# Three extra 8-column matmuls in a gated attention and mLSTM layer

## The chip, the cores and the metric

The kernel runs on 1 core of one Trainium2 chip. The metric is the device time of one execution in microseconds (us); less is better. The TensorE clock granted in the profiled execution was 0.999 of full speed.

## What is computed

One layer of a hybrid network on 256 tokens of width 1024, in float32. The input is normalized and modulated to `h`, and one large product `h @ w_in` gives 13 pieces: attention's queries, keys, values and gate input `za`; the mixer's (mLSTM's) `qm`, `km`, `vm`, `zm`, `om` and its two small gates; and the two output gates `ga` and `gm`. Cut to what matters here:

```python
h = _rmsnorm(x, norm_w) * (1 + scale) + shift
(qa, ka, va, za, qm, km, vm, zm, om, ig, fg, ga, gm) = jnp.split(h @ w_in, SPLIT_IDX, axis=-1)
ya = merge(_moba_attention(qa, ka, heads(va, ATT_HEADS), rel_bias))
ya = (ya * jax.nn.silu(za)) @ w_att_proj
...
ym = (merge(hm).astype(x.dtype) * jax.nn.silu(zm)) @ w_ml_proj
y = jax.nn.sigmoid(ga) * ya + jax.nn.sigmoid(gm) * ym
return x + gate * (y @ w_out)
```

## The kernel before

**The products.** Each float32 operand is split into a high part (`wh`, `hTh`) that TensorE's one-pass float32 format (`F32R`) holds exactly, and a low part (`wl`, `hTl`) with the rest. A product is then three matmuls: high by high, high by low, low by high. ScalarE (ACT) makes `wh` from the loaded block (line 449), VectorE (DVE) or GpSimd (POOL) makes `wl` by a subtraction (line 453).

**The chunks.** After a first phase (lines up to 300) the work is a list of chunks of 512 output columns, two per piece ("halves"), in the order ka, va, za, qm, km, att, zm, vm, om, ga, gm, ml, out. A chunk has 4 steps, which I call groups; a group covers 2 of the 8 blocks of 128 rows over which the product sums. There are two kinds of interest:

- "tok" chunks (lines 1087 to 1089) stream 512 columns of weights for each loaded block of `h`;
- "ws" chunks (za, qm, km, att, ga, gm, ml; lines 1094 to 1097) load a 128 by 128 block of weights and stream the 256 tokens of `h`. For each of the 2 blocks of the sum and each of 4 column blocks `i`, three matmuls stand in a row: `wh` with `hTh` (line 1094), `wh` with `hTl` (line 1096), `wl` with `hTh` (line 1097). That is 24 matmuls a group, each with its own weight load (LDWEIGHTS).

**The order.** The order on every engine is written out by hand: at step `g` the loop over groups first splits the weights of a later group (`HB` = 5 buffers ahead), then runs the hooks that are listed for that step, then issues the group's matmuls. Hooks put other work of TensorE between groups: attention's scores and transposes (lines 695, 696, 720 to 722) and its products with the values (733, 735) ahead of groups of va, za and the first groups of qm; the mixer's products (852 to 854) ahead of the second, third and fourth group of ga; transposes of the mixer's result (892) ahead of gm's first group and ahead of the first group of its second half. I call such a piece an interlude. The result of a ws chunk goes to a PSUM tile `mm` of 128 by 4 by 256 words, one slice for each `i`, with two such tiles in turn.

Of the kernel before, what the change touches and what calls it, by code (L numbers as in the profile page):

```python
# [64 lines left out]
def tile_hybrid(ctx: ExitStack, tc: tile.TileContext, x, c, params, params2, rel_t, w_row, ada_mod, ada_gate,  # L65
                w_in, w_att_proj, w_ml_proj, w_out, out):
    nc = tc.nc
# [212 lines left out]
    for step in P1_STEPS:  # L280
        op, k = step[0], int(step[1])
# [16 lines left out]

    chunks = []

    STRASSEN = ('zm', 'om')

    def seg(kind, src, c0, name, stat=None):
        if name in STRASSEN:
            chunks.append(dict(kind="str", src=src, c0=c0, half=0, n=512, name=name, stat=stat))
            return
        for hf in range(2):
            chunks.append(dict(kind=kind, src=src, c0=c0, half=hf, n=512, name=name, stat=stat))
# [20 lines left out]
    NG = len(owner)  # L329
    for nm in STRASSEN:  # L330
        C[nm, 1] = C[nm, 0]

    def start(name, half=0):
        return step0[C[name, half]]

    def done(name, half):
        return step0[C[name, half]] + (14 if name in STRASSEN else 4)

# [119 lines left out]
    def at(step, fn, *a):  # L458
        hooks.setdefault(step, []).append((fn, a))
# [527 lines left out]
    for i, j in enumerate((0, 1, 2, 3)):  # L987
        at(start("qm") + 2 + 4 * i, left_split, j)
    for nm in STRASSEN:
        s = start(nm)  # L990
# [4 lines left out]
    for hp in range(2):  # L995
        s = done("om", hp)
        if "om" in STRASSEN:
            for i in range(2):
# [17 lines left out]
    mmt = {}  # L1016
# [16 lines left out]
    for g in range(NG):  # L1033
        ci = owner[g]
        kp = g - step0[ci]
        ch = chunks[ci]
# [29 lines left out]
        sh_, sl_ = (hTh, hTl) if ch["stat"] is None else (T[stat[ch["stat"]][0]], T[stat[ch["stat"]][1]])  # L1066
        wh, wl = whl[g]
        if ci == NCH - 1:
            continue
        if ch["kind"] == "str":  # L1070
            p = kp // 2
            o = mmt[ci][(0, 2, 0, 1, 0, 2, 0)[p]]
            for kk in range(2):
                k = 2 * (kp % 2) + kk
# [5 lines left out]
        for kk in range(2):  # L1080
            k = 2 * kp + kk
            first, last = k == 0, k == KT - 1
            if ch["kind"] == "tok":
                for t in range(2):
                    a, b = sh_[:, k, t * 128:(t + 1) * 128], sl_[:, k, t * 128:(t + 1) * 128]
                    o = mmt[ci][:, t, 0:ch["n"]]
                    nc.tensor.matmul(o, a, wh[:, kk], start=first, stop=False)  # L1087
                    nc.tensor.matmul(o, a, wl[:, kk], start=False, stop=False)  # L1088
                    nc.tensor.matmul(o, b, wh[:, kk], start=False, stop=last)  # L1089
            else:  # L1090
                for i in range(4):
                    cs = slice(i * 128, (i + 1) * 128)
                    o = mmt[ci][:, i]
                    nc.tensor.matmul(o, wh[:, kk, cs], sh_[:, k], start=first and i % 2 == 0, stop=False,  # L1094
                                     skip_group_check=True)
                    nc.tensor.matmul(o, wh[:, kk, cs], sl_[:, k], start=False, stop=False, skip_group_check=True)  # L1096
                    nc.tensor.matmul(o, wl[:, kk, cs], sh_[:, k], start=False, stop=last and i % 2 == 1,  # L1097
                                     skip_group_check=True)
    ci = NCH - 1
    for t, c0, n in ((0, 0, 512), (1, 0, 256), (1, 256, 256)):  # L1100
        pt = ps.tile([128, n], F32, name="mm", bufs=2)
        for k in range(KT):
            wh, wl = whl[step0[ci] + k // 2]
            wh, wl = wh[:, k % 2, c0:c0 + n], wl[:, k % 2, c0:c0 + n]
# [52 lines left out]
```

## Time and profile before

| | |
|---|---|
| median of 3 runs | 350.89 us (350.68 to 351.04) |
| the profiled execution | 350.94 us |
| its span, first to last instruction | 349.2 us |
| TensorE matmuls busy | 343.6 us, 2320 matmuls and as many weight loads |
| VectorE, ScalarE, GpSimd busy | 270.7, 228.1, 104.9 us |
| matmuls in ws chunks | 1344 of 256 columns (320 + 64 + 64 at each of lines 1094, 1096, 1097) |

The busy time of a matmul in the profile overlaps that of its neighbours, since matmuls are pipelined; a row's duration of 276 ns does not mean that a matmul takes a slot of 276 ns. What a matmul costs in a stream is the distance from its start to the next one's start, and this is read from the timeline's start column.

### The profile page before, as it was taken

What the parts mean: (1) busy time and instruction counts of PE and PEld (TensorE: products, weight loads), DVE (VectorE), ACT (ScalarE), POOL (GpSimd) and SP (SyncE); (2) the same over time, 40 slices, a digit from 0 to 9 for tenths busy, and PEclk for the clock granted to TensorE, in tenths of its full rate; (3) what the DMA queues carried; (4) which work ended last, traced back from release to release, by engine and by line L of the source; (5) the groups of instructions that cost most, each with busy time, mean ns of one, the idle gap of its engine ahead of it and who ended that gap; (6) DMA issues with size and microseconds to landing.
All of it is one profiled execution on the core that took longest, in us unless ns stands there. A gap on an engine that the chain in (4) does not pass through costs nothing.

```text
span 349.2 us, 6004 instructions
## 1 busy us (share of the span) xinstructions
PE 343.6 (98%) x2320; PEld 315.0 (90%) x2320; DVE 270.7 (78%) x392; ACT 228.1 (65%) x355; POOL 104.9 (30%) x102
## 2 busy tenths in 40 slices
PE   8999999999999999999999999999999999999995
PEld 4988889888999999999999888888899999999885
DVE  4799994897984445668699897999966889888772
ACT  3777787989977678676644985469956425834410
POOL 4940003765202999744714000100003440000000
PEclk9999999999999999999999999999999999999999
DMA  8999999995483063275398484957969029746011
GB/s 299 418 419 420 417 381 344 243 259 229 140 286 122 11 246 129 98 287 198 103 333 167 158 326 145 363 95 274 387 231 354 20 94 321 312 174 249 0 62 60
DMA packets 26782, 80.05 MB, mean 229 GB/s; under 512 B 2045, under 2 KB 5121, under 8 KB 26242
## 3 DMA queue, kind: packets, MB, share of 16 engines
q1 hardware_dynamic: 25392, 77.03, 61.2%
q0 software_dynamic: 1056, 2.10, 3.5%
q10 hardware_dynamic: 306, 0.55, 0.5%
q8 instruction: 18, 0.29, 0.3%
q14 instruction: 10, 0.08, 0.1%
HBM read 78.22 MB, written 1.45 MB: 228 GB/s over the span
## 4 chain that ended last, share of the span: by engine, by line
PE 82%; DMA 8%; POOL 4%; DVE 2%; ACT 2%; issue 1%; SPq 0%; DVEq 0%; POOLq 0%; ACTq 0%
PE mm L1094 15%; PE mm L1097 15%; PE mm L1096 15%; DMA raw<-in_w_row_dram 8%; PE pm L186 4%; PE mm L1087 4%; PE mm L1089 4%; PE mm L1088 4%; PE aux L1076 4%; PE aux L1077 4%; PE aux L1078 4%; POOL ms L572 2%; PE mm L1108 1%; PE mm L1106 1%; PE mm L1107 1%
## 5 line engine op out<-in xcount | busy, mean ns | idle before, releaser
L453 DVE TENSOR_TENSOR wl<-raw,wh 128x1024 fp32r<-128x1024 f32 (+1 forms) x96 | 118.4, 1255 | 32.6 <-ACT wh L449 32.5
L449 ACT CAST wh<-raw 128x1024 fp32r<-128x1024 f32 (+1 forms) x104 | 104.7, 1031 | 26.4 <-PE mm L1096 15.1
L1094 PE MATMUL mm<-hTh,wh 128*128 128x256 f32 x320 | 89.9, 281 | 0.0
L1097 PE MATMUL mm<-hTh,wl 128*128 128x256 f32 x320 | 89.0, 278 | 0.0
L1096 PE MATMUL mm<-hTl,wh 128*128 128x256 f32 x320 | 89.0, 278 | 0.0
L1094 PEld LDWEIGHTS mm<-hTh,wh 128*128 128x128 f32 x320 | 60.4, 189 | 0.0
L1097 PEld LDWEIGHTS mm<-hTh,wl 128*128 128x128 f32 x320 | 60.3, 188 | 0.0
L1096 PEld LDWEIGHTS mm<-hTl,wh 128*128 128x128 f32 x320 | 60.2, 188 | 0.0
L1087 PE MATMUL mm<-wh,hTh 128*128 128x512 f32 (+1 forms) x96 | 36.3, 378 | 0.0
L1089 PE MATMUL mm<-wh,hTl 128*128 128x512 f32 (+1 forms) x96 | 35.7, 372 | 0.0
L1088 PE MATMUL mm<-wl,hTh 128*128 128x512 f32 (+1 forms) x96 | 35.7, 372 | 0.0
L1089 PEld LDWEIGHTS mm<-wh,hTl 128*128 128x128 f32 x96 | 18.0, 188 | 3.2
L1088 PEld LDWEIGHTS mm<-wl,hTh 128*128 128x128 f32 x96 | 18.1, 188 | 2.9
L1087 PEld LDWEIGHTS mm<-wh,hTh 128*128 128x128 f32 x96 | 18.0, 188 | 2.8
L453 POOL TENSOR_TENSOR wl<-raw,wh 128x1024 fp32r<-128x1024 f32 x8 | 20.0, 2533 | 0.0
L175 DVE TENSOR_TENSOR wrl<-raw,wrh 128x512 fp32r<-128x512 f32 (+1 forms) x24 | 18.2, 778 | 1.6 <-ACT wrh L170 1.3
L1094 PE MATMUL mm<-yah,wh 128*128 128x256 f32 x64 | 17.9, 279 | 0.0
L170 ACT CAST wrh<-raw 128x512 fp32r<-128x512 f32 (+1 forms) x24 | 15.8, 685 | 3.1 <-DMA raw<-in_w_row_dram 3.1
L1096 PE MATMUL mm<-yal,wh 128*128 128x256 f32 x64 | 17.7, 276 | 0.0
L1097 PE MATMUL mm<-yah,wl 128*128 128x256 f32 x64 | 17.7, 276 | 0.0
L1097 PE MATMUL mm<-ymh,wl 128*128 128x256 f32 x64 | 17.7, 276 | 0.0
L1094 PE MATMUL mm<-ymh,wh 128*128 128x256 f32 x64 | 17.7, 276 | 0.0
(237 smaller groups left out, 773.6 us busy)
## 6 DMA issues: line engine op xcount, KB each, us to landing
raw<-in_w_in_dram SPq DMA_DIRECT2D x36, 1024.0 KB, 5.4
adat<-in_ada_mod_dram SPq DMA_DIRECT2D x16, 512.0 KB, 9.4
raw<-in_w_att_proj_dram SPq DMA_DIRECT2D x4, 1024.0 KB, 5.0
gw<-in_ada_gate_dram SPq DMA_DIRECT2D x4, 1024.0 KB, 8.6
raw<-in_w_ml_proj_dram SPq DMA_DIRECT2D x4, 1024.0 KB, 7.5
raw<-in_w_out_dram SPq DMA_DIRECT2D x4, 1024.0 KB, 8.9
raw<-in_w_row_dram SPq DMA_DIRECT2D x4, 896.0 KB, 12.6
raw<-in_w_row_dram SPq DMA_DIRECT2D x4, 640.0 KB
```

The costliest lines, as they stand in the source:

```text
L170: copy(wsp[k][0][:, c0:c1], wrow[k][:, c0:c1])
L175: e.tensor_tensor(l[:, cs], wrow[k][:, cs], h[:, cs].bitcast(F32), op=OP.subtract)
L186: nc.tensor.matmul(pm[ch][:, t], a[:, k, t * 128:(t + 1) * 128], b[:, cs], start=k == 0 and i == 0 and (ch < 3 or t == 0), stop=k == KT - ...
L449: nc.scalar.copy(h, w)
L453: e.tensor_tensor(l, w, h.bitcast(F32), op=OP.subtract)
L1076: nc.tensor.matmul(o, a, wh[:, kk], start=k == 0 and p in (0, 1, 3), stop=False, skip_group_check=True)
L1087: nc.tensor.matmul(o, a, wh[:, kk], start=first, stop=False)
L1088: nc.tensor.matmul(o, a, wl[:, kk], start=False, stop=False)
L1089: nc.tensor.matmul(o, b, wh[:, kk], start=False, stop=last)
L1094: nc.tensor.matmul(o, wh[:, kk, cs], sh_[:, k], start=first and i % 2 == 0, stop=False, skip_group_check=True)
L1096: nc.tensor.matmul(o, wh[:, kk, cs], sl_[:, k], start=False, stop=False, skip_group_check=True)
L1097: nc.tensor.matmul(o, wl[:, kk, cs], sh_[:, k], start=False, stop=last and i % 2 == 1, skip_group_check=True)
```

## The change

A table names three pieces and a position for each. In the first half of such a piece, at the first of its 96 matmuls (`k` = 0, `i` = 0), one more matmul is issued: the same weights `wh`, and the first 8 of the 256 columns of `hTh`. In za it stands ahead of the first matmul and writes to the first 8 words of slice 0; in ga behind the first, in gm behind the second, both into the first 8 words of slice 2. Each of these words is started afresh by a later matmul, so nothing of the extra product stays in the result.

```diff
+    EXTRA = {'za': 1, 'ga': 2, 'gm': 3}
...
                     o = mmt[ci][:, i]
+                    extra = EXTRA.get(ch["name"]) if first and i == 0 and ch["half"] == 0 else None
+                    if extra == 1:
+                        nc.tensor.matmul(o[:, 0:8], wh[:, kk, cs], sh_[:, k, 0:8], start=True, stop=True,
+                                         skip_group_check=True)
                     nc.tensor.matmul(o, wh[:, kk, cs], sh_[:, k], start=first and i % 2 == 0, stop=False,
                                      skip_group_check=True)
+                    if extra == 2:
+                        nc.tensor.matmul(mmt[ci][:, 2, 0:8], wh[:, kk, cs], sh_[:, k, 0:8], start=True, stop=True,
+                                         skip_group_check=True)
                     nc.tensor.matmul(o, wh[:, kk, cs], sl_[:, k], start=False, stop=False, skip_group_check=True)
+                    if extra == 3:
+                        nc.tensor.matmul(mmt[ci][:, 2, 0:8], wh[:, kk, cs], sh_[:, k, 0:8], start=True, stop=True,
+                                         skip_group_check=True)
                     nc.tensor.matmul(o, wl[:, kk, cs], sh_[:, k], start=False, stop=last and i % 2 == 1,
                                      skip_group_check=True)
```

The added lines shift the numbers below them: lines 1094, 1096, 1097 of before are 1099, 1104, 1108 of the changed kernel, and lines between the table and there move by one. The other engines' instructions and waits stay as they are, and so do the waits on TensorE.

TensorE at the start of za, in the changed kernel: behind the three transposes of attention (`aux<-ident,P`) the extra matmul (128x8) is the first of the chunk.

```order
L721 MATMUL aux<-ident,P 128x128 [waits DVE_49,Activation_49]
L722 MATMUL aux<-ident,P 128x128
L723 MATMUL aux<-ident,P 128x128
L1097 MATMUL mm<-hTh,wh 128x8
L1099 MATMUL mm<-hTh,wh 128x256
L1104 MATMUL mm<-hTl,wh 128x256
L1108 MATMUL mm<-hTh,wl 128x256
```

In the kernel before, the row of line 1097 with 128x8 is not there, and the others stand in the same order. None of the ws rows has a wait there.

TensorE at the start of gm's first half, before: eight transposes of the mixer's result (the last two shown as one row), then the chunk's matmuls. Only the first waits (for ACT, which makes `wh`).

```order
L892 MATMUL aux<-ident,omt 128x128 [waits DVE_49]
L892 MATMUL aux<-ident,omt 128x128 x2
L1094 MATMUL mm<-hTh,wh 128x256 [waits Activation_49]
L1096 MATMUL mm<-hTl,wh 128x256
L1097 MATMUL mm<-hTh,wl 128x256
```

And the same place in the changed kernel:

```order
L893 MATMUL aux<-ident,omt 128x128 [waits DVE_49]
L893 MATMUL aux<-ident,omt 128x128 x2
L1099 MATMUL mm<-hTh,wh 128x256 [waits Activation_49]
L1104 MATMUL mm<-hTl,wh 128x256
L1106 MATMUL mm<-hTh,wh 128x8
L1108 MATMUL mm<-hTh,wl 128x256
```

The extra matmul has gone between the second and the third, and no wait has moved. For comparison, the first group of gm's second half, which the change does not touch, starts like this in the kernel before: its third matmul does wait (for DVE, which makes `wl`).

```order
L892 MATMUL aux<-ident,omt 128x128 x8
L1094 MATMUL mm<-hTh,wh 128x256 [waits Activation_49]
L1096 MATMUL mm<-hTl,wh 128x256
L1097 MATMUL mm<-hTh,wl 128x256 [waits DVE_49]
L1094 MATMUL mm<-hTh,wh 128x256
```

In ga the extra matmul stands between the first (which waits for ACT) and the second matmul of the chunk, behind a last matmul of om with 512 columns.

## The prediction, on record before the changed kernel ran

> **What bounds the kernel now.** First the page's line of busy times, then the list of what TensorE (PE) waited for, then the timeline's last rows.
>
> ```profile
> PE 343.6 (98%) x2320; PEld 315.0 (90%) x2320; DVE 270.7 (78%) x392; ACT 228.1 (65%) x355; POOL 104.9 (30%) x102
> ```
>
> ```profile
> PE warm L213 <- POOL ident masks.py:199: 1.4, 1, 1.4
> PE pc L220 <- DMA xnT<-in_c_dram: 0.3, 1, 0.3
> ```
>
> ```profile
> 345.54 0.42 DVE L932 TENSOR_TENSOR o<-mm,gateb 128x256 f32<-128x256 f32 x1 [1.99 <-PE mm L1108]
> ```
>
> TensorE is busy all the time, waits for nobody beyond the first few microseconds, and its last matmul releases the last evacuation. So the time is the sum of TensorE's slots, and a slot saved or added anywhere from 12 us on is saved or added at the end: no other engine covers it, and none comes late when TensorE gains a few tenths (no wait of its own is left to grow).
>
> The rest of the argument is about the length of a slot. I read how many ws matmuls start in stretches of 10 us without an interlude (the windows view: the stretch, its length, busy time and count of matmuls, of weight loads, of DVE, ACT and POOL, then the granted clock and the DMA share).
>
> ```profile
> 147.00:157.00 10.00, 10.00 (x91) 10.00 (x90) 7.05 (x13) 6.81 (x11) 5.26 (x3) 1.00 0.66 246
> 279.00:289.00 10.00, 10.00 (x88) 10.00 (x87) 8.47 (x11) 3.21 (x7) 3.84 (x1) 1.00 0.32 108
> ```
>
> The same instructions, at the same granted clock (1.00), run at two rates. Starts of whole groups of 24 matmuls, from the timeline, give the sizes: in gm's first half (281.22 on) and in its second (293.32 on).
>
> ```profile
> 281.22 0.28 PE L1094 MATMUL mm<-hTh,wh 128*128 128x256 f32 x1
> ...
> 284.05 0.28 PE L1094 MATMUL mm<-hTh,wh 128*128 128x256 f32 x1
> ```
>
> ```profile
> 293.32 0.28 PE L1094 MATMUL mm<-hTh,wh 128*128 128x256 f32 x1
> ...
> 296.04 0.28 PE L1094 MATMUL mm<-hTh,wh 128*128 128x256 f32 x1
> ```
>
> A slow group takes 284.05 - 281.22 = 2.83 us (118 ns a matmul), a fast one 296.04 - 293.32 = 2.72 us (113 ns): 0.11 us lie between them. Read so over the whole timeline, 16 of the 56 ws groups are slow: all 8 of za and the first 2 of qm, ga's first and third, and the 4 of gm's first half. Inside a stretch the rate does not change after the first few matmuls; it is chosen anew behind an interlude. Two entries of the same kind, both behind eight transposes:
>
> ```profile
> 277.29 0.28 PE L1096 MATMUL mm<-hTl,wh 128*128 128x256 f32 x1
> 277.40 0.28 PE L1097 MATMUL mm<-hTh,wl 128*128 128x256 f32 x1
> 277.52 1.04 PE L892 MATMUL aux<-ident,omt 128*128 128x128 f32 x8
> 278.31 0.36 PE L1094 MATMUL mm<-hTh,wh 128*128 128x256 f32 x1
> 278.51 0.28 PE L1096 MATMUL mm<-hTl,wh 128*128 128x256 f32 x1
> 278.63 0.28 PE L1097 MATMUL mm<-hTh,wl 128*128 128x256 f32 x1
> 278.75 0.28 PE L1094 MATMUL mm<-hTh,wh 128*128 128x256 f32 x1
> ```
>
> ```profile
> 290.50 0.37 PE L1094 MATMUL mm<-hTh,wh 128*128 128x256 f32 x1
> 290.70 0.28 PE L1096 MATMUL mm<-hTl,wh 128*128 128x256 f32 x1
> 290.82 0.28 PE L1097 MATMUL mm<-hTh,wl 128*128 128x256 f32 x1
> 290.94 0.28 PE L1094 MATMUL mm<-hTh,wh 128*128 128x256 f32 x1
> 291.05 0.28 PE L1096 MATMUL mm<-hTl,wh 128*128 128x256 f32 x1
> 291.17 0.28 PE L1097 MATMUL mm<-hTh,wl 128*128 128x256 f32 x1
> ```
>
> The first stays slow for four groups; the second is fast from its fourth matmul on. What differs in the program is that the third matmul of the second entry waits for DVE. In the program's order the third matmul has a wait at three more entries behind plain float32 products, in qm and att:
>
> ```profile
> 126.11 0.37 PE L1094 MATMUL mm<-hTh,wh 128*128 128x256 f32 x1
> ...
> 166.83 0.37 PE L1094 MATMUL mm<-yah,wh 128*128 128x256 f32 x1
> ...
> 180.34 0.37 PE L1094 MATMUL mm<-yah,wh 128*128 128x256 f32 x1
> ```
>
> All three begin fast stretches. The seven entries in za (87.55, below, is the first) have no wait there, like 278.31, and all are slow. I take from this that a small upset of the order of load and matmul at an entry moves TensorE from the slow rhythm to the fast one. It is not certain: behind the streams in one-pass format in ga, the rate is slow, fast, slow, fast without such a rule.
>
> **The change part by part.** *What an extra matmul costs.* The trace has no 8-column matmul in this format. Nearest is the pair of 36-column transposes at 106.14, a short matmul behind which the next weight load stands bare, and the durations of the load rows.
>
> ```profile
> 106.14 0.31 PE L678 MATMUL aux<-ident,GE 36*128 36x36 f32 x2
> ```
>
> ```profile
> L678 PEld LDWEIGHTS aux<-ident,GE x2: 136/137/138, 106.1 to 106.2; 36*128 36x128 f32 x2
> L678 PE MATMUL aux<-ident,GE x2: 227/238/248, 106.1 to 106.2; 36*128 36x36 f32 x2
> ```
>
> ```profile
> L1094 PEld LDWEIGHTS mm<-hTh,wh x320: 187/188/193, 87.5 to 301.0; 128*128 128x128 f32 x160
> ```
>
> The pair lasts 0.31 us in all and its second one at least 0.227, so the step between them is 0.08 us: the lower end. A load in ws chunks reads 188 ns against 137 there, 0.05 us more; 0.08 + 0.05 = 0.13 us is the upper end. I take one fast slot, 0.11 us, which lies between and is what a weight load that no matmul hides would add if it is as long as the slot. Three of them cost 0.33 us (0.25 to 0.40). All lies on the path, for nothing else bounds. The Trainium skill (TensorE: Matmul & The Clock Gate, LDWEIGHTS) counts a load by its columns, P / 1.2 ns; for 128 columns that is an estimate of 107 ns, or 0.32 us for three. The step of 0.08 us with 128 weight columns is under that figure, so for transposes the trace does not bear it out; for ws loads no run here has shown it bare.
>
> *What an extra matmul can save.* It repeats weights that are loaded before or after it, and its 8 columns are over long before the next load is, so the next matmul must wait for its weights: an upset at the entry, larger than that which the wait at 290.50 makes. If it tips the stretch into the fast rhythm, gm's first half gains four groups, 4 x 0.11 = 0.44 us. In za the extra matmul acts on the first group alone, since the next interlude begins behind it and the entry there is as before: 0.11 us. In ga too: only the first group is slow up to the next interlude, 0.11 us.
>
> ```profile
> 87.55 0.36 PE L1094 MATMUL mm<-hTh,wh 128*128 128x256 f32 x1
> ...
> 90.47 0.38 PE L695 MATMUL aux<-kT,qT 128*128 128x256 f32 x1
> ```
>
> ```profile
> 251.19 0.28 PE L1094 MATMUL mm<-hTh,wh 128*128 128x256 f32 x1
> ...
> 254.02 0.28 PE L852 MATMUL aux<-vaug,SD 128*128 128x258 f32 x1
> ```
>
> *Sum, all three tipped:* 0.33 - 0.44 - 0.11 - 0.11 = -0.33 us. The profiled execution took 350.94 us (span 349.2), 0.05 above the median of 350.89; against the median that is 350.56, which I round to **350.6**. In za and ga the extra pays back just its own cost (0.11 against 0.11); the gain is gm's (0.44 - 0.11). With gm alone tipped: 0.33 - 0.44 = -0.11, 350.8.
>
> No wait is added, no DMA and no other engine's instruction moves; the words that the extra matmul writes are in PSUM tiles that the chunk's own first matmuls already wait for. These edits cost nothing beyond the slot.
>
> **The rivals.**
>
> *Nothing tips.* The rhythm could hang on something that 8 columns do not touch. Then the three slots are all there is: +0.33 us, 351.2. For it: three entries in ga differ without a cause that I can name. Against: waits of a few nanoseconds do seem to tip it. The Trainium skill (same page, Back-to-back issue gap) gives the distance of matmuls by their columns alone, N / 2.4 + 2.5 ns, and knows no second rhythm; by that rule each matmul is only a cost and this rival would hold. The trace disagrees with the rule in that 256 columns take 113 and 118 ns at one clock, where it gives 109.
>
> *The rhythm outlives the interludes.* If a fast first group of za carried over the interludes, za's other 7 groups and qm's first 2 would become fast as well (9 x 0.11 = 0.99 us), and in ga the third group (0.11): -0.33 - 1.10 = -1.43 us, 349.5. Against it speaks the fence that begins at 277.29: ga's last group still runs at 277.40 - 277.29 = 0.11 us a matmul, and eight transposes later the rate is slow. So for that interlude it is refuted; those of za are others.
>
> *The ga stretch breaks.* This is the one that ends slower. ga's second group and its last five are fast now without a wait that would make them so (the entry to the last five has none at its third matmul). The extra matmul shifts the phase at which the mixer's products and then these groups begin. If those six groups fall into the slow rhythm (6 x 0.11 = 0.66 us) and nothing tips, the sum is 0.33 + 0.66 = +0.99 us, 351.9. It decides for "slower" from four such groups on: 0.33 + 4 x 0.11 = 0.77.
>
> **How the numbers follow.** Tipping of gm, with or without za and ga: 0.50, and 350.4 to 350.9 by the bounds of the slot (3 x 0.03 us each way) and the two small terms. Nothing tips: 0.20. Outliving: 0.20. The ga stretch breaks: 0.10. A measurement of this kernel can tell about 0.2%, 0.70 us, from no change. The first two cases lie within it, outliving is faster, the broken stretch slower; a little of the first two I move outward for combinations (some interludes outlived, some of ga's groups lost): faster 0.22, same 0.66, slower 0.12. The range reaches from outliving (349.5, with 0.1 for the slot's lower bound: 349.4) to nothing tipped at the slot's upper bound (350.94 + 0.40 = 351.3, with one more group lost 351.4); the broken stretch is left out.
>
> **What the new profile would show.** Right: 3 more matmuls and loads (x2323); in gm's first half group starts 2.72 us apart and about 91 matmuls in 10 us; in za the first group 2.72 + 0.11 us long and the following ones still 2.83; in ga the first group likewise, and groups four to eight as before. The start behind each 8-column matmul comes 0.08 to 0.13 us after it. Wrong: gm's groups still 2.83 us apart (nothing tips); za's later groups at 2.72 (outliving); ga's last five at 2.83 (broken); or a wait of TensorE in its list that was not there, since the whole sum rests on there being none.

## The result and the profile after

The changed kernel takes 353.34 us (median of 4 runs, 353.23 to 353.93) against 350.94 us for the kernel before (4 runs, 350.68 to 351.04): a ratio of 1.0076, 95% interval 1.0060 to 1.0092. It is slower by 0.76%, and the forecast of 350.6 us (349.4 to 351.4) was wrong. The profiled execution took 353.43 us, its span is 351.6 us against 349.2.

TensorE still sets the time. Its line of the page, and the list of what it waited for:

```profile
PE 346.3 (98%) x2323; PEld 317.2 (90%) x2323; DVE 271.2 (77%) x392; ACT 228.6 (65%) x355; POOL 108.6 (31%) x102
```

```profile
PE warm L213 <- POOL ident masks.py:199: 1.4, 1, 1.4
```

Three matmuls and three loads more, and no wait that was not there. So the loss is in the length of the slots. The entry of za (timeline: start, duration, operation):

```profile
87.11 0.27 PE L723 MATMUL aux<-ident,P 128*128 128x128 f32 x1
87.14 0.25 PE L1097 MATMUL mm<-hTh,wh 128*128 128x8 f32 x1
87.25 0.36 PE L1099 MATMUL mm<-hTh,wh 128*128 128x256 f32 x1
87.45 0.28 PE L1104 MATMUL mm<-hTl,wh 128*128 128x256 f32 x1
...
88.60 0.28 PE L1108 MATMUL mm<-hTh,wl 128*128 128x256 f32 x1
...
89.96 0.28 PE L1108 MATMUL mm<-hTh,wl 128*128 128x256 f32 x1
```

The 256-column matmul starts 0.11 us behind the 8-column one, and the twelve matmuls from 88.60 on take 1.36 us, 113 ns each: za is now fast, all eight groups of it. But km is slow, and so are gm's second half and ml (windows view, columns as in the prediction; first the kernel before in the second stretch, where it was fast, then the changed kernel in both):

```profile
295.00:305.00 10.00, 10.00 (x91) 10.00 (x90) 8.46 (x12) 6.67 (x9) 0.00 (x0) 1.00 0.84 334
```

```profile
147.00:157.00 10.00, 10.00 (x87) 10.00 (x87) 7.05 (x13) 7.29 (x11) 5.27 (x4) 1.00 0.72 272
295.00:305.00 10.00, 10.00 (x87) 10.00 (x86) 8.46 (x13) 5.62 (x8) 0.00 (x0) 1.00 0.91 349
```

The two rates, measured over the whole of ml, from its first matmul to the first 512-column one behind its 192; first before, then after:

```profile
301.48 0.28 PE L1094 MATMUL mm<-ymh,wh 128*128 128x256 f32 x1
...
323.24 0.40 PE L1087 MATMUL mm<-wh,hTh 128*128 128x512 f32 x1
```

```profile
303.12 0.28 PE L1099 MATMUL mm<-ymh,wh 128*128 128x256 f32 x1
...
325.74 0.40 PE L1088 MATMUL mm<-wh,hTh 128*128 128x512 f32 x1
```

21.76 / 192 = 113.3 ns and 22.62 / 192 = 117.8 ns, both at a granted clock of 1.00. The 8 groups of ml took 0.86 us longer, so a slow group costs 0.107 us more than a fast one (0.855 / 8, from the unrounded starts).

A map shows where they lie. One letter stands for a ws group, in the order of the program; F is a mean step of 113 ns between its matmuls, S one of 118, read from the timeline:

```
         za       qm       km       att      ga       gm   ml         slow
before   SSSSSSSS SSFFFFFF FFFFFFFF FFFFFFFF SFSFFFFF SSSSFFFF FFFFFFFF  16
after    FFFFFFFF FFSSSSSS SSSSSSSS SSSSSSSS SFSFFFFF SSSSSSSS SSSSSSSS  40
```

(gm has two halves of four groups; ml follows without anything between.) The sum: za and qm's first two groups give 10 x 0.107 = -1.07 us; the rest of qm, km and att cost 22 x 0.107 = +2.35; gm's second half and ml 12 x 0.107 = +1.28; three slots 3 x 0.11 = +0.33. In all 24 slow groups more and three slots, +2.90 us. To measure it without what lies ahead of za (za begins between 86.9 and 88.0 us in the runs below, though nothing ahead of it is changed), I take the time from za's first matmul to the program's last. The last one, before and after:

```profile
345.22 0.28 PE L1108 MATMUL mm<-wh,hTl 128*128 128x256 f32 x1
```

```profile
347.71 0.28 PE L1119 MATMUL mm<-wh,hTl 128*128 128x256 f32 x1
```

345.22 - 87.55 = 257.67 us before, 347.71 - 87.14 = 260.57 after: +2.90 us (+2.91 from unrounded starts). The account is closed; what is left to explain is why the rhythm is what it is.

One more row gives the slow rhythm a name. In a fast group every weight load reads 187 or 188 ns; in a slow one, one load of every three reads 192. Loads in gm's first half before, in its first half after, and in its second half after (line and operation, count, duration in ns min/median/max):

```profile
L1097 PEld LDWEIGHTS mm<-hTh,wl x24: 192/192/192, 281.3 to 289.5; 128*128 128x128 f32 x24
L1094 PEld LDWEIGHTS mm<-hTh,wh x23: 187/188/188, 281.5 to 289.2; 128*128 128x128 f32 x23
L1096 PEld LDWEIGHTS mm<-hTl,wh x23: 187/188/188, 281.6 to 289.4; 128*128 128x128 f32 x23
```

```profile
L1104 PEld LDWEIGHTS mm<-hTl,wh x23: 192/192/192, 282.1 to 289.9; 128*128 128x128 f32 x23
```

```profile
L1099 PEld LDWEIGHTS mm<-hTh,wh x28: 192/192/192, 293.1 to 302.7; 128*128 128x128 f32 x28
```

The three matmuls of a (k, i) are the first (line 1094 before), the second (1096) and the third (1097). The long load is on the third in the one, on the second in the other: the first half of gm is as slow as it was, but not in the same state. I call the states fast, slow-1, slow-2 and slow-3 by the load that is long. ga's first group, too, is as slow as before, and there the long load has gone from the second of the three to the first.

### The profile page after: what moved, and what is told of

Same layout as the page of the kernel before. It is cut to its first block, busy times and chain, and to the rows that moved or that the text cites. A ratio compares the mean times of both kernels' runs of the same rounds, so it can differ in the third digit from the quotient of the medians.

```text
span 351.6 us, 6010 instructions
## 1 busy us (share of the span) xinstructions
PE 346.3 (98%) x2323; PEld 317.2 (90%) x2323; DVE 271.2 (77%) x392; ACT 228.6 (65%) x355; POOL 108.6 (31%) x102
## 4 chain that ended last, share of the span: by engine, by line
PE 82%; DMA 8%; POOL 4%; DVE 2%; ACT 2%; issue 1%; SPq 0%; DVEq 0%; POOLq 0%; ACTq 0%
PE mm L1104 15%; PE mm L1099 15%; PE mm L1108 15%; DMA raw<-in_w_row_dram 8%; PE pm L186 4%; PE mm L1090 4%; PE mm L1089 4%; PE mm L1088 4%; PE aux L1078 4%; PE aux L1079 4%; PE aux L1077 4%; POOL ms L573 2%; PE mm L1119 1%; PE mm L1117 1%; PE mm L1118 1%
## 5 line engine op out<-in xcount | busy, mean ns | idle before, releaser
L269 POOL COPY rvec<-relT 8x1 f32<-8x1 f32 (+11 forms) x32 | 18.1, 620 | 0.0
```

The costliest lines, as they stand in the source:

```text
L269: nc.gpsimd.tensor_copy(rvec[:, m0:m1], relT[:, b:b + 1].to_broadcast([AH, m1 - m0]))
```

## The experiments

All kernels at once: the map, the slow groups, the time worked out (0.107 us for each slow group against before's 16, 0.111 for each short matmul) and the time measured from za's first matmul to the last matmul, less before's 257.67. "Short" is an 8-column matmul like those of the change (in the runs with a table `SHORT` of positions it takes the weights of the matmul that it stands ahead of). A "?" is a group that changes inside.

```
                     za       qm       km       att      ga       gm   ml         slow  sum    measured
after                FFFFFFFF FFSSSSSS SSSSSSSS SSSSSSSS SFSFFFFF SSSSSSSS SSSSSSSS  40   +2.90  +2.91
e1  za's alone       FFFFFFFF FFSSSSSS SSSSSSSS SSSSSSSS SFSFFFFF SSSSFFFF FFFFFFFF  28   +1.40  +1.44
e2  two in za        FFFFFFFF FFSSSSSS SSSSSSSS SSSSSSSS SFSFFFFF SSSSFFFF FFFFFFFF  28   +1.51  +1.55
e3  za, transpose    SSSSSSSS SSFFFFFF FFFFFFFF FFFFFFFF SFSFFFFF SSSSFFFF FFFFFFFF  16      -    0.00
e4  za, 256 columns  SSSSSSSS SSFFFFFF FFFFFFFF FFFFFFFF SFSFFFFF SSSSFFFF FFFFFFFF  16   +0.12  +0.12
e5  ahead of gm      SSSSSSSS SSFFFFFF FFFFFFFF FFFFFFFF SFSFFFFF FFFFSSSS SSSSSSSS  24   +0.97  +0.97
e6  za, ahead of qm3 FFFFFFFF FFSSSSSS SSSSSSSS SSSSSSSS SFSFFFFF SSSSFFFF FFFFFFFF  28   +1.51  +1.55
e7  za, in qm3       FFFFFFFF FFSSSSSS SSSSSSSS SSSSSSSS SFSFFFFF SSSSFFFF FFFFFFFF  28   +1.51  +1.55
e8  gm's alone       SSSSSSSS SSFFFFFF FFFFFFFF FFFFFFFF SFSFFFFF SSSSSSSS SSSSSSSS  28   +1.40  +1.37
e9  waits moved, 2   FFFFFFFF FFSSSSSS SSSSSSSS SSSSSSSS SFSFFFFF FFFFSSSS SSSSSSSS  36   +2.36  +2.41
e10 waits moved      SSSSSSSS SSFFFFFF FFFFFFFF FFFFFFFF SFSFFFFF SSSSFFFF FFFFFFFF  16    0.00   0.00
e11 za, 512 at qm3   FFFFFFFF FFSSSSSS SSSSSSSS SSSSSSSS SFSFFFFF SSSSFFFF FFFFFFFF  28   +1.62  +1.67
e12 three in gm      SSSSSSSS SSFFFFFF FFFFFFFF FFFFFFFF SFSFFFFF SSSFSSSS SSSSSSSS  27   +1.51  +1.52
e13 two in gm        SSSSSSSS SSFFFFFF FFFFFFFF FFFFFFFF SFSFFFFF SSSSSSSS SSSSSSSS  28   +1.51  +1.48
e14 one in qm1       SSSSSSSS FFSSSSSS SSSSSSSS SSSSSSSS SFSFFFFF SSSSFFFF FFFFFFFF  36   +2.25  +2.23
e15 two in qm1       SSSSSSSS FFSSSSSS SSSSSSSS SSSSSSSS SFSFFFFF SSSSFFFF FFFFFFFF  36   +2.36  +2.37
e16 za, late in qm3  FFFFFFFF FF?FFFFF FFFFFFFF FFFFFFFF SFSFFFFF SSSSFFFF FFFFFFFF   6   -0.79  -0.63
e17 za, pairs apart  FFFFFFFF FFFFFFFF FFFFFFFF FFFFFFFF SFSFFFFF SSSSFFFF FFFFFFFF   6   -0.96  -0.81
e18 pairs apart      SSSSSSSS SSFFFFFF FFFFFFFF FFFFFFFF SFSFFFFF SSSSFFFF FFFFFFFF  16    0.00  +0.01
```

(e11's sum has 0.23 us for its 512-column matmul; e16's counts half of the group with the "?". In za a fast group saves 0.09 rather than 0.107 us, since the first matmuls of each go at the same pace; that is part of the 0.15 by which the last sums are off.) The map and the number of shorts give the time of every kernel to within 0.16 us. Most kernels have one run, but this stretch repeats well: before, e3, e10 and e18, with the same map and no short in it, agree to 0.01 us, where the whole times of before reach from 350.39 to 351.59 us. So no time hides anywhere else, and the rest of the work is about the map.

### Which piece does what: e1 and e8

za's extra alone, and gm's alone:

```diff
-    EXTRA = {'za': 1, 'ga': 2, 'gm': 3}
+    EXTRA = {'za': 1}
```

```diff
-    EXTRA = {'za': 1, 'ga': 2, 'gm': 3}
+    EXTRA = {'gm': 3}
```

> Only za's extra matmul is left; the two of ga and gm are gone. Theory 'count': each extra weight load of this kind, wherever it stands, swaps the slow and the fast rhythm of every stretch behind it, until the next extra one swaps them again. Then za's groups and qm's first two are fast, the rest of qm, km and att slow, and, unlike in the changed kernel, ga and gm are swapped against the kernel before: ga's groups 1 and 3 fast, 2 and 4 to 8 slow, gm's first half fast, its second half and ml slow. 40 slow groups against 16 before: 24 x 0.107 + 0.08 = +2.6 us, about 353.5. Rival 'local': an extra matmul sets the rhythm anew only where it stands, and what came behind ga and gm in the changed kernel was the work of their own extras. Then 28 slow groups, ga, gm and ml as before: 12 x 0.107 + 0.08 = +1.4 us, about 352.3.

> Only gm's extra matmul is left, behind the second matmul. Theory 'carried': a bare weight load changes the rhythm from its place on, and the changed rhythm is carried over later interludes until something else changes it. Then gm's extra alone makes gm's second half and ml slow, 12 groups more, and leaves the rest as in the kernel before: 28 slow groups, 12 x 0.107 + 0.11 = +1.4 us over the kernel before. Rival 'joint': the slow second half needs the extras of za or ga as well; then 16 slow groups and +0.11 us.

e1 took 352.06 us (before 351.59 in the same session, one run each), e8 352.19 (before 350.80). In the profile of e1, km is slow and ml fast; in that of e8 the other way round (windows view):

```profile
147.00:157.00 10.00, 10.00 (x87) 10.00 (x86) 7.05 (x13) 7.23 (x11) 5.26 (x4) 1.00 0.73 278
295.00:305.00 10.00, 10.00 (x91) 10.00 (x90) 8.46 (x13) 5.64 (x8) 0.00 (x0) 1.00 0.91 356
```

```profile
147.00:157.00 10.00, 10.00 (x91) 10.00 (x90) 7.05 (x14) 6.91 (x11) 5.26 (x3) 1.00 0.67 243
295.00:305.00 10.00, 10.00 (x87) 10.00 (x87) 8.46 (x12) 6.17 (x9) 0.00 (x0) 1.00 0.77 300
```

The two effects are apart and add up to the map of the changed kernel. Each extra makes slow a stretch that begins far behind it and that it doesn't touch: za's at the third group of qm, 37 us later, gm's at the gate's second half, 12 us later. Nothing that follows ga's first group hangs on ga's extra: besides its slot, it moved the long load within that group.

### What in za's extra does it: e2, e3, e4

Two shorts instead of one; a 128x128 transpose in its place; the same matmul with all 256 columns. In e2 to e4 za's is the only extra.

```diff
-                    if extra == 1:
+                    for _ in range(2 if extra == 1 else 0):
```

```diff
-                        nc.tensor.matmul(o[:, 0:8], wh[:, kk, cs], sh_[:, k, 0:8], start=True, stop=True,
-                                         skip_group_check=True)
+                        nc.tensor.transpose(o[:, 0:128], ident, ident)
```

```diff
-                        nc.tensor.matmul(o[:, 0:8], wh[:, kk, cs], sh_[:, k, 0:8], start=True, stop=True,
+                        nc.tensor.matmul(o, wh[:, kk, cs], sh_[:, k], start=True, stop=True,
```

> Two extra 8-column matmuls ahead of za, none in ga and gm. Theory 'count': two swaps cancel, every stretch has the rhythm of the kernel before (16 slow groups), and only two slots are added: +0.16 to +0.2 us, about 351.1. Rival 'local' (the short matmul upsets the entry): za becomes fast and qm to att slow as with one extra, 352.3 or more.

> One extra 128x128 transpose ahead of za in place of the 8-column matmul, none in ga and gm. In the kernel before, attention's interludes hold three transposes each, an odd number, and yet all entries in za are alike; so by 'count' transposes do not count: rhythm as before, +0.11 us, about 351.05. Rival 'place': what counts is the number of instructions in TensorE's queue (a transpose is also one load and one matmul), so it swaps like the 8-column matmul: za fast, 40 slow groups, about 353.5.

> The extra matmul ahead of za has all 256 columns, none in ga and gm: the next weight load is hidden behind it, as behind every other matmul. Theory 'count': the width is of no matter, rhythms as with the 8-column one in za alone, 40 slow groups, one full slot more: +2.7 us, about 353.6. Rival 'bare load' (the step of the prediction: the next matmul must wait for its weights, and this upset tips the rhythm): no upset, rhythm as before, +0.11 us, about 351.05.

They took 352.51, 350.72 and 351.45 us (before 351.59). Two shorts act like one, so it isn't whether the number of loads is odd or even. A transpose or a full matmul leaves every rate as in before, so it isn't only that the instructions behind stand one place further on. They do move the long load in za's first group, from the third of the three to the first in e3 and to the second in e4; the second group is slow-1 in all three kernels. Lines 1097 of before and 1104 of e4, in za's first group:

```profile
L1097 PEld LDWEIGHTS mm<-hTh,wl x7: 192/192/193, 88.1 to 90.2; 128*128 128x128 f32 x7
```

```profile
L1104 PEld LDWEIGHTS mm<-hTl,wh x6: 192/192/192, 88.8 to 90.6; 128*128 128x128 f32 x6
```

What makes za fast is the matmul with 8 columns and not the same one with 256. That it acts because it is too short to cover the load that follows it fits this, but no width between was run.

### Shorts at other entries: e5, e6, e7

A table says at which of the 24 matmuls of a group a short stands ahead (0 is ahead of the first, 3 behind the third):

```diff
+    SHORT = {('gm', 0, 0): (0,)}
...
+                    short(0)
                     nc.tensor.matmul(o, wh[:, kk, cs], sh_[:, k], start=first and i % 2 == 0, stop=False,
                                      skip_group_check=True)
+                    short(1)
                     nc.tensor.matmul(o, wh[:, kk, cs], sl_[:, k], start=False, stop=False, skip_group_check=True)
+                    short(2)
```

e6 has `{('za', 0, 0): (0,), ('qm', 0, 2): (0,)}`, e7 `{('za', 0, 0): (0,), ('qm', 0, 2): (3,)}`.

> One extra 8-column matmul, in gm as in za: ahead of the first matmul, behind the same kind of transposes. Theory 'position': what an extra does hangs on the kind of work around it; ahead of the chunk it makes gm's first half fast (4 groups less, -0.43 us), as it did in za, and by the carrying the second half and ml slow (12 groups more): +1.29 - 0.43 + 0.11 = +1.0 us over the kernel before. Rival 'tips to fast' (the prediction's): the first half fast and the second half, whose third matmul waits, fast as before: -0.43 + 0.11 = -0.3 us. Rival 'no difference of position': as behind the second matmul, first half slow, second half and ml slow: +1.4 us.

> Za's extra ahead, and a second one ahead of the first matmul of qm's third group (first half), where the rhythm turned slow in the run with za's alone; it writes to the next chunk's PSUM tile. Theory 'carried': the second extra changes the rhythm once more, and the 22 groups to the end of att are fast again: 6 slow groups in all (ga 1 and 3, gm's first half), 10 x 0.107 = -1.07 + 0.22 = -0.85 us against the kernel before. Rival 'the wait decides': the third matmul there waits for DVE, and behind a carried fast rhythm this wait turns it slow whatever stands ahead: 28 slow groups, +1.4 + 0.11 us.

> As the run before, with the second extra behind the third matmul of that group, so behind the waiting one. 'Carried': again a change, slow to fast, -0.85 us against the kernel before with 6 slow groups. Rival 'position': inside a running stretch an extra leaves or makes it slow, as in ga and gm: 28 slow groups or more, +1.5 us.

351.86, 352.02 and 352.39 us (before 350.80). Ahead of gm, behind eight transposes, a short makes the first half fast, as in za, and then the second half and ml go slow: a gain of 4 groups turned into a loss of 12. At qm's third group, behind the products of attention and values, a short does not bring the fast rhythm back, neither ahead nor three matmuls in. In e6 the long load stays on the first of three, as in e1. In e7 it stands on the third, through the rest of qm and all of km; its loads up to 158 us:

```profile
L1114 PEld LDWEIGHTS mm<-hTh,wl x84: 192/192/192, 128.7 to 158.0; 128*128 128x128 f32 x84
```

### The prediction's rule, the wait on the third matmul: e10 and e9

The product with the low part of the weights is issued first at the four entries where the third matmul waits, so that the wait stands on the first; e9 has shorts ahead of za and of gm as well.

```diff
+                    three = [(wh, sh_), (wh, sl_), (wl, sh_)]
+                    if here and (ch["name"], ch["half"], kp) in LOW_FIRST:
+                        three = three[2:] + three[:2]
+                    for j, (w, m) in enumerate(three):
+                        nc.tensor.matmul(o, w[:, kk, cs], m[:, k], start=first and i % 2 == 0 and j == 0,
+                                         stop=last and i % 2 == 1 and j == 2, skip_group_check=True)
```

> The four first triples with wl first, no extra matmul at all. 'A wait on the third matmul turns it': without it the slow rhythm goes on: qm, km, att slow as well (22 groups more) and gm's second half and ml (12 more), 50 slow groups, 34 x 0.107 = +3.6 us against the kernel before. Rival 'the interlude turns it': 16 slow groups, no change of time.

> Extras of 8 columns ahead of za and ahead of gm's first half. And in the four groups behind an interlude whose third matmul waits (qm's third group, the first groups of att's two halves and of gm's second half), the first triple is issued with wl first, so that the wait stands on the first matmul and none on the third. Theory 'carried, and a wait on the third matmul turns it': the extras make za and gm fast, nothing turns the rhythm, and all stretches but ga's groups 1 and 3 are fast: 2 slow groups, 14 x 0.107 = -1.50 + 0.22 = -1.3 us against the kernel before, 0.37% faster. Rival 'the interlude turns it': not the wait but the work ahead of these groups (products with the values, mixer's products, transposes) turns a carried fast rhythm; then qm from its third group, att, gm's second half and ml are slow: 36 slow groups, 20 x 0.107 + 0.22 = +2.4 us.

e10 took 350.61 us and its map is before's, letter for letter. e9 took 353.11 us (median of 4; before 350.8, 7 runs; ratio 1.0060, 1.0043 to 1.0077), turned at the same places as e1 and e5. The entry to gm's second half in e10, with no wait on its third matmul, has the pace of the prediction's rows from 290.50 on, 0.20, 0.12, 0.12 and 0.11 us from start to start:

```profile
290.17 0.37 PE L1110 MATMUL mm<-hTh,wl 128*128 128x256 f32 x1
290.37 0.28 PE L1110 MATMUL mm<-hTh,wh 128*128 128x256 f32 x1
290.49 0.28 PE L1110 MATMUL mm<-hTl,wh 128*128 128x256 f32 x1
290.61 0.28 PE L1110 MATMUL mm<-hTh,wh 128*128 128x256 f32 x1
290.72 0.28 PE L1110 MATMUL mm<-hTl,wh 128*128 128x256 f32 x1
```

The wait on the third matmul has no part in it.

### A long matmul at the turn: e11

```diff
+    WIDE = (('qm', 0, 2),)
...
+                        nc.tensor.matmul(mmt[ci + 1][:, 0:2], wh[:, kk, cs], sh_[:, k:k + 2], start=True, stop=True,
+                                         skip_group_check=True)
```

> Za's 8-column extra, and ahead of qm's third group one extra matmul of 512 columns, which lasts twice as long as a weight load and so lets the loads get ahead again; it writes to the next chunk's PSUM tile. Theory 'what is carried is the lead of the loads': the 512 columns restore it, as the 512-column chunks between att and ga seem to, and from here on all is as in the kernel before: za fast, 6 slow groups, 10 x 0.107 = -1.07 + 0.11 + 0.23 = -0.7 us. Rival: the lead is not it, one long matmul restores nothing: 28 slow groups, +1.3 + 0.34 = +1.6 us.

352.47 us: qm stays slow from its third group on (the long load is now on the second of the three there, on the first in e1). One 512-column matmul does not restore the fast rhythm.

### The long load moves by steps: e12, e13, e14, e15

Shorts inside a running slow stretch. `SHORT` is `{('gm', 0, 0): (2, 5), ('gm', 0, 3): (2,)}` in e12, `{('gm', 0, 0): (2, 5)}` in e13, `{('qm', 0, 0): (2,)}` in e14 and `{('qm', 0, 0): (2, 5)}` in e15.

> Before with three 8-column matmuls in the first half of mixer's gate and none elsewhere: behind the second and the fifth or so matmul of its first group (each behind the second of a three) and behind the second of its last group. In a slow stretch one load of each three takes 192 ns, the others 188. Theory 'position' (the long load comes at every third load counted through, the extra ones too, so each short shifts it by one in the program's three, and the position at the end of the first half decides what the transposes between the halves do): three shifts are none, the first half ends with the long load on the third of each three as in before, and the second half and the last projection are fast; 16 slow groups, the time of before and 3 slots of 0.11 us, +0.3 us. Rival 'the short' (a short in the first half spoils the turn, however many): second half and last projection slow, 28 slow groups, +1.3 us for them and +0.3 for the slots.

> Before with two 8-column matmuls in the first group of mixer's gate, behind the second and the fifth matmul (each behind the second of a three). 'Position': the long load is shifted by two, to the first of each three, a position that no run has shown at this place; the second half may be either, and the long load stands on the first of each three in the whole first half. 'The short': the second half and the last projection slow, +1.3 us and two slots of 0.11 us; where the long load stands is not said.

> Before with one 8-column matmul in the first group of mixer's q, behind its second matmul, two groups ahead of the third group, where before turns from slow to fast. There the long load is on the first of each three in before. 'Position': it shifts to the third of each three, and the third group may then stay slow, as the gate's second half did on another position; if it does, mixer's q, its k and the attention projection are slow, 22 more groups, +2.3 us and 0.11 for the slot. 'The short sets the rhythm only where it follows transposes': nothing is changed but the slot, +0.1 us, and the third group turns fast.

> As the kernel with one short in the first group of mixer's q, with a second one behind the fifth matmul. 'Position': the long load shifts by two, to the second of each three, ahead of the third group; what the third group does then may differ from what one short gives (slow where that was fast, or the other way). 'The short sets the rhythm only where it follows transposes': third group fast as in before, +0.2 us for the slots.

352.36, 351.86, 352.94 and 353.20 us (before 351.07, one run each). Three shorts are not as none, so "position" fell as it was put. But the load rows show what each short does. In e13 two shorts put the long load on the first of the three (line 1109), and the second half then on the third (1114):

```profile
L1109 PEld LDWEIGHTS mm<-hTh,wh x21: 192/192/192, 281.8 to 288.9; 128*128 128x128 f32 x21
```

```profile
L1114 PEld LDWEIGHTS mm<-hTh,wl x22: 192/192/192, 293.9 to 301.3; 128*128 128x128 f32 x22
```

In e12 the same two come first, and the third short, in the last group, makes that group fast: no load is long any more. The second half is then slow with the long load on the second of three (line 1112):

```profile
L1114 PEld LDWEIGHTS mm<-hTh,wl x6: 187/188/188, 287.9 to 289.6; 128*128 128x128 f32 x6
L1109 PEld LDWEIGHTS mm<-hTh,wh x5: 187/188/188, 288.0 to 289.4; 128*128 128x128 f32 x5
L1112 PEld LDWEIGHTS mm<-hTl,wh x5: 187/188/188, 288.1 to 289.5; 128*128 128x128 f32 x5
```

```profile
L1112 PEld LDWEIGHTS mm<-hTl,wh x23: 192/192/192, 293.9 to 301.7; 128*128 128x128 f32 x23
```

In e14 one short in qm's first group, which is in slow-1, makes that group and the next fast, and the third group turns to slow:

```profile
L1112 PEld LDWEIGHTS mm<-hTl,wh x11: 187/188/188, 119.5 to 122.9; 128*128 128x128 f32 x11
...
```

```profile
L1109 PEld LDWEIGHTS mm<-hTh,wh x29: 192/192/192, 127.9 to 137.8; 128*128 128x128 f32 x29
```

So each short that stands ahead of the third matmul of a three moves the state one step: slow-3, slow-2 (one short: the changed kernel, e8), slow-1 (two: e13), fast (three: e12; from slow-1 one: e14), and a second short in fast changes nothing (e15). The changed kernel's short in ga, ahead of the second of a three, took slow-2 to slow-1, one step as well. e7's stands ahead of the first of a three and took slow-1 to slow-3, not to fast: the step may hang on the place in the three, or on the products ahead of it, and no run parts the two.

What stands between two stretches takes each state to a certain one. The eight transposes ahead of gm's second half: slow-3 to fast (before and every kernel with gm's first half untouched), slow-2 to slow-1 (changed kernel, e8), slow-1 to slow-3 (e13), fast to slow-2 (e5, e9, e12). The two pairs of products ahead of qm's third group: slow-1 to fast (before), fast to slow-1 (e1, e14, e15). The mixer's scores ahead of att's first half (lines 832 and 835 of before): fast stays fast (before), and slow-1 (e1), slow-2 (e11) and slow-3 (e7) all come out as slow-3. Only one of the four states comes out fast at gm's second half, and before happens to be in it; one or two or three shorts there spoil it.

### Two kernels that are faster than before: e16, e17, and e18

If that holds, one short in the slow-1 stretch behind qm's turn, ahead of the third of a three, should make the rest fast (e16: `{('za', 0, 0): (0,), ('qm', 0, 2): (14,)}`). The other way is to take the turn away: e17 has za's short and the second pair of products one group later; e18 has that move alone, without any short.

```diff
-        at(done("za", 1) + 2, att_av, 4 + 2 * q)
+        at(done("za", 1) + 2 + q, att_av, 4 + 2 * q)
```

> Before with one 8-column matmul ahead of attention's z, as the change has it, and one more in the third group of mixer's q, behind its 14th matmul, when the slow rhythm has settled. Theory 'steps' (in a settled slow stretch each short moves the rhythm one step along: long load on the third of three, on the second, on the first, fast; in a fast one it changes nothing): the third group is entered slow with the long load on the first, the short makes it fast, and mixer's q, k and the attention projection stay fast. 6 to 7 slow groups instead of 16, -1.0 us, two slots of 0.11 us, in all -0.8 us. Rival 'only behind transposes' (a short makes fast only where it follows transposes): 28 slow groups as with za's extra alone, +1.5 us.

> Before with one 8-column matmul ahead of attention's z, and the second of the two pairs of attention x values products at the third group of mixer's q moved one group later. One pair by itself, ahead of the sixth and the seventh group of za, leaves a fast rhythm fast in the changed kernel. Theory 'composition' (each stretch of other work turns the rhythm by a rule of its own, one pair leaves fast fast): mixer's q, its k and the attention projection fast, 6 slow groups instead of 16, -1.07 us and +0.11 for the slot, in all -1.0 us. Rival 'the place' (it is turned at the third group whatever stands there, or at the fourth): 28 slow groups as with za's extra alone, +1.4 us.

> Before with nothing but the second of the two pairs of attention x values products at the third group of mixer's q moved one group later. In za of before one pair takes the slow rhythm with the long load on the first of three to slow with it on the second, and the next pair back. 'Composition': mixer's q stays slow from there, its k and the attention projection too, 38 slow groups instead of 16, +2.35 us. 'The place': third or fourth group turns fast as in before, no change in time.

e16: 350.32 us (median of 10, 349.87 to 350.87) against 350.84 (16 runs, 350.39 to 351.43), ratio 0.9983 (0.9974 to 0.9993). e17: 350.09 us (7 runs, 349.47 to 350.67), ratio 0.9977 (0.9965 to 0.9989). e18: 350.87 us, one run. A stretch of km (windows view) of e16, e17 and e18, and the first and last matmul of e17:

```profile
147.00:157.00 10.00, 10.00 (x91) 10.00 (x90) 7.05 (x14) 6.62 (x12) 5.27 (x4) 1.00 0.66 238
```

```profile
147.00:157.00 10.00, 10.00 (x91) 10.00 (x90) 7.05 (x13) 7.38 (x11) 5.26 (x4) 1.00 0.78 280
```

```profile
147.00:157.00 10.00, 10.00 (x91) 10.00 (x90) 7.05 (x14) 6.94 (x11) 5.27 (x3) 1.00 0.66 236
```

```profile
86.91 0.25 PE L1097 MATMUL mm<-hTh,wh 128*128 128x8 f32 x1
...
343.76 0.28 PE L1119 MATMUL mm<-wh,hTl 128*128 128x256 f32 x1
```

343.76 - 86.91 = 256.85 us, 0.81 less than before's 257.67 (rounded rows). Both kernels that were meant to keep za's gain and lose the turn did so. e16 bears out the steps. In e17 one pair at a time leaves fast fast, twice, where the two pairs together turn it to slow-1. In e18 the "composition" as it was put went wrong: the single pair at the third group turned slow-1 to fast. The place in za that the expectation leaned on is not the same work, as the timeline of before shows ahead of za's seventh group:

```profile
110.62 0.27 PE L720 MATMUL aux<-ident,P 128*128 128x128 f32 x1
110.73 0.27 PE L721 MATMUL aux<-ident,P 128*128 128x128 f32 x1
110.84 0.27 PE L722 MATMUL aux<-ident,P 128*128 128x128 f32 x1
110.95 0.60 PE L733 MATMUL aux<-PT,vat 128*128 128x256 f32 x2
```

There three transposes stand ahead of the pair. e17's expectation leaned on the same places in za, so that it came out right is in part luck. A pair alone takes slow-1 and fast both to fast; two pairs in one, slow-1 to fast and fast to slow-1. It was luck of this kind, not the wait, that made qm fast in before.

## Why the prediction was wrong

**What bounds.** Right. TensorE is busy 98% of the span, waits for nobody, and the sum of its slots closes to 0.01 us (+2.90 worked out, +2.91 measured between the first matmul of za and the last).

**What an extra matmul costs.** Right: 0.11 us was taken, with 0.08 to 0.13 as bounds. In za the next matmul starts 0.11 us behind (87.14, 87.25), as was foretold for all three. In gm it starts 0.03 us behind, and the delay stands one matmul later (timeline):

```profile
279.63 0.28 PE L1104 MATMUL mm<-hTl,wh 128*128 128x256 f32 x1
279.75 0.17 PE L1106 MATMUL mm<-hTh,wh 128*128 128x8 f32 x1
279.78 0.36 PE L1108 MATMUL mm<-hTh,wl 128*128 128x256 f32 x1
279.98 0.28 PE L1099 MATMUL mm<-hTh,wh 128*128 128x256 f32 x1
```

From the second matmul to the first of the next three are 0.35 us where two slow slots are 0.24: 0.11 for the short. The Trainium skill (TensorE: Matmul & The Clock Gate, LDWEIGHTS) counts a load as P / 1.2 ns, an estimate of 107 ns for 128 columns; the slot of a short in this format, 0.111 us, agrees with that within a few ns.

**What an extra matmul can save: the step that failed.** "In za the extra matmul acts on the first group alone, since the next interlude begins behind it and the entry there is as before." Behind it stood the reading that the rate "is chosen anew behind an interlude". The entries of za's later groups are as before in the program, and they are fast all the same. The state is carried over the interludes of za; a stretch's rate is not chosen by its own entry alone. The sum priced za at 0.11 us and nothing downstream. What hung on za's state was 10 groups gained and 22 lost, +1.28 us net. The same error again in gm: the sum stopped at the end of its first half, and 12 groups behind it were lost, +1.28 us. The gains of the sum failed too, all but one: gm's -0.44 and ga's -0.11 came out as nothing, since gm's first half and ga's first group stayed slow; za's -0.11 came, with nine groups more. Of the 3.24 us between the forecast -0.33 and the measured +2.91, gm's missing gain makes 0.44, ga's 0.11, and the stretches behind za's first group and gm's first half 2.7 (25 slow groups net).

**The rule.** That "a small upset of the order of load and matmul at an entry moves TensorE from the slow rhythm to the fast one" was read off four entries with a wait on the third matmul. Two of them, att's halves, show nothing: km and att are fast ahead of them as well as behind. e10 moved the wait, and all four entries stayed as they were, down to the pace of their first matmuls. They were places with their own state and their own interlude; nothing in the trace of before had varied the wait while the rest stood still. A short ahead of the first matmul does make fast behind transposes (za, and e5 for gm), and so far za's first group became fast as forecast. But gm's extra stands behind the second matmul, and there it only moved the long load from the third of three to the second.

**The rivals.** "The rhythm outlives the interludes" had the mechanism of za right: seven more groups of za and qm's first two did become fast. It was priced as a gain only, because carried on was read as carried on fast. The fence at 277.29 was read as its refutation: ga's last groups are fast, gm's first half slow. The rows fit an interlude that turns the state as well as one that wipes it: every kernel here comes to this place fast, and without a short there leaves it in slow-3, so which it is stays open. At gm's second half, where four states arrive, each leaves as another, and at qm's third group slow turns to fast and fast to slow: these turn. A state that is carried and turned there makes fast ahead of the turn into slow behind it. This reversed form of the rival, with all it reaches, would have been 10 gained against 22 lost.

"The ga stretch breaks" did not happen: ga is SFSFFFFF in every kernel here. Between att and ga stand the long 512-column chunks, and whether att ends fast or in slow-3, ga begins in slow-2. The Trainium skill's distance between matmuls by columns alone (same page, Back-to-back issue gap) has neither of the two rates, 113.3 and 117.8 ns at full granted clock. The Trainium skill calls that formula the gap of a single matmul and says that in a stream of loads and matmuls both set the spacing, which the prediction left out. Three slots as the whole price, as in "Nothing tips", leave out 2.57 of the 2.90 us.

**What stays open.** Shown: there are four states, a short ahead of the third of a three moves them by a step, transposes and products between stretches take a state to another or leave it, and the time is the count of slow groups. Not shown: what the states are. In both rhythms the loads run one ahead of their matmuls (a matmul starts 110 ns behind its own load in a fast group, 114 to 115 in a slow one), and which part of TensorE or of its reads goes through a cycle of three loads no run here could tell. Nor is it known why a short at the entry behind the two pairs (e6, e7) does not follow the steps, or what in an interlude decides where it takes each state: one pair of products and two treat fast differently, and the same eight transposes take fast to slow-3 ahead of gm's first half (every kernel without a short there) and to slow-2 ahead of its second (e5, e9, e12). For a kernel not yet run, nothing here lets one work out the map from the program.

## What to carry to other kernels

Where one engine bounds a kernel, and equal instructions at an equal granted clock run at two rates, make the map of rates by group over the whole program first, and ask of a change not only what it does where it stands but what state it hands on: here 0.33 us of added matmuls made the kernel 2.4 us slower, by stretches that begin 12 and 37 us behind them. A regularity over a few entries (a wait here, none there) is a guess until one run has moved that one thing. Such a state is cheap to try: one profile shows the map, and stretches ahead of an edit had the same map in every kernel here, so the sum of the slots then gives the time from the first edit on to a tenth or two of a microsecond.

## What the runs showed of the hardware

TensorE streams 256-column matmuls of this format at 113.3 or at 117.8 ns a step, at a granted clock of 1.00 in both. In the slow one, one weight load of three takes 192 ns and the others 187 or 188; in the fast one all take 187 or 188. The state lasts through whole stretches (64 threes of matmuls in ml without a change) and over other work. An 8-column matmul costs a slot of 0.11 us and can change the rate, there and in later stretches. A 256-column one costs its slot of 0.12 us (e4), and a transpose behind transposes took 0.11 us ahead of za's first matmul (87.19 to 87.30 in e3); both moved the long load in za's first group, and neither changed any group's rate.
